# A transformer layer with 32 routed experts on one core: the last experts in another order, the accumulator's rows added after the last product, norm statistics on two engines, bounded row transfers

## The chip, the core and the metric

One core of one Trainium2 chip runs the whole layer in one launch. Its engines work side by side and meet at semaphores: TensorE (PE; its weight loads are listed as PEld), VectorE (DVE), ScalarE (ACT), GpSimd (POOL) and SyncE (SP). In this kernel SP issues the plain DMAs and POOL the indirect ones, in which a list of row numbers says which rows of a DRAM tensor are gathered or scattered. Sixteen DMA engines carry all of them. The metric is the time of one execution in microseconds (us); lower is better.

## The reference, cut to what matters

A batch of 512 tokens of width 1024 goes through a token mixer (differential attention beside a gated MLP), a LayerNorm, a mixture of experts and a second LayerNorm. The change concerns the last two:

```python
logits = xt @ w_router + b_router                      # 512 tokens, 32 experts
topv, topi = lax.top_k(logits, 4)
gates = softmax(topv)
for each expert e, for its tokens:
    h = xb @ w_up[e] + b_up[e]                         # 1024 -> 2 x 1024
    gate, lin = h[:, :1024], h[:, 1024:]
    act = (clip(lin, -7, 7) + 1) * min(gate, 7) * sigmoid(1.702 * min(gate, 7))
    y = act @ w_down[e] + b_down[e]                    # 1024 -> 1024
ffn = sum over a token's 4 experts of gate * y
x = layer_norm(2**0.25 * x + ffn, ln2_g, ln2_b)        # the output
```

There are 512 x 4 = 2048 pairs of a token and an expert.

## The kernel before, in words

**Slots.** The experts are sorted on the chip by how many tokens they have, and every rank has a fixed capacity (`CAP_STEPS`); slot 0 is a fixed expert with 128 rows. A rank of at most 64 rows is an L, of 65 to 128 an M, of 129 to 192 an H (an M of 128 rows plus an L of 64). The capacities of the 32 ranks sum to 2976 rows. `ORDER` says in which order the 31 sorted ranks follow slot 0; each letter takes the largest rank of its kind that is left. The last slot must be an L.

**An expert's work.** The up product writes PSUM tiles PG and PL, the down product PD (or X1 for the L part of an H, and for an L that stands ahead of an H). An M multiplies in three passes (L1359) of weights that ACT casts (L152) and DVE subtracts (L153) into five `ring` buffers; an L multiplies its 64 rows with the raw weights (L1345), two column halves at a time. TensorE's order is fixed by a list of chunks: up of slot n, then down of slot n-1, and at the end down of slot 30, up of slot 31, down of slot 31. Events hang between chunks: lists and gathers, transposes, activations, outputs.

**Weights.** An expert's 12 MiB come in six DMAs of 2 MiB from SP, each into one of six `raw` buffers, and a load goes out when the buffer that is six loads older has been used up.

**Rows.** `gather` (L869) and `gather_h` (L1176) fetch a slot's token rows from `x1d`; `scatter` (L1228) and `scatter_h` (L1181) add its results to `accd`, the accumulator in DRAM. Lists are as long as the capacity; entries without a token name one of 128 spare rows behind the 512 real ones, so 2976 rows are moved each way. Scatters follow one another: each waits until the one ahead has landed. The results stand in two buffers `ys` until their scatter has read them.

**The end.** When the scatter of slot 30 is issued, `summed` gathers the rows of `accd` that the last expert's tokens have (`accr`, L1625) and loads all of `accd` (`xo`, L1629, four tiles of 128 rows). `last_start` (L1690) puts `accr` into PD by two pairs of matmuls with the identity, ahead of the last down product; since that sum must be weighted right, the last expert's activations are multiplied by the gates when they are transposed (`gated`, L1295, with `last_diag`, `last_mm`, `last_gates`), and its list (`full_list`) repeats a real token in empty places. ACT forms the norm's sums (L1642) and squares (L1651) of the four `xo` tiles; DVE scales them (L1657), finishes them (L764) and SP stores them (L1665). `last_rows` then norms the last expert's rows: statistics from PD (L1696), a matmul that joins the two halves of a row (L1699), a reciprocal square root of one column in eight DVE steps, two DVE operations (L1711, L1712) and a scatter into the output (L1713), which has to come after the stores, as it overwrites rows of theirs. A loop for overflowing experts follows (L1757), here with no trips.

Of the kernel before, what the change touches and what calls it, by code (L numbers as in the profile page):

```python
# [11 lines left out]
I32 = mybir.dt.int32  # L12
# [7 lines left out]
S = 512  # L20
# [36 lines left out]
ORDER = "LMLHLMLMLMLHLMLMLMLHLMLMMLMLHLL"  # L57
# [10 lines left out]
def moe_layer(ctx, tc, x, w_in, lambda_q1, lambda_k1, lambda_q2, lambda_k2, subln_g, gmlp_ln_g,  # L68
# [786 lines left out]

    def list_cols(lp, rows, dst=None):
# [317 lines left out]
    def gather_h(idx):  # L1174
        xg = xgs[nxt("xg", len(xgs))][:, 0:512]
        nc.gpsimd.indirect_dma_start(out=xg, out_offset=None, in_=x1d_h,  # L1176
# [17 lines left out]

    def full_list(s):

        lp = xbank()[:, 0:8].rearrange("p (n c) -> p n c", n=2)
        for n in range(2):
            for i in range(NT):
                cols = tb.oh[:, i, 0:1].to_broadcast([128, 128]) if n else tb.oh[:, i]  # L1200
                nc.tensor.matmul(lp[:, n], cols, tb.R[:, i, s], start=(n == 0 and i == 0), stop=(n == 1 and i == 3))
        cols_ = words("r0", 16)
        t = view(cols_, 0, 2, 4)
        empty, gt, idx = (view(cols_, 8 + n, 1) for n in range(3))
        idx = idx.bitcast(I32)
        nc.vector.tensor_copy(t, lp)
        nc.vector.tensor_scalar(empty, t[:, 0, 1:2], -1.0, 1.0, op0=OP.mult, op1=OP.add)
        nc.vector.scalar_tensor_tensor(t[:, 0], t[:, 1], empty, t[:, 0], op0=OP.mult, op1=OP.add)
        nc.vector.scalar_tensor_tensor(idx, t[:, 0, 0:1], 2.0, bge[:, 2:3], op0=OP.mult, op1=OP.add)
        nc.vector.tensor_tensor(gt, t[:, 0, 2:3], t[:, 0, 3:4], op=OP.add)  # L1210
        return idx, gt
# [15 lines left out]
    def scatter(y, idx):  # L1227
        nc.gpsimd.indirect_dma_start(out=accd, out_offset=bass.IndirectOffsetOnAxis(ap=idx, axis=0),  # L1228
                                     in_=y, in_offset=None, compute_op=OP.add)
# [3 lines left out]
    class Slot:  # L1233
# [34 lines left out]
        def fetch(self, b):  # L1268
            if self.last:
                self.lists[b] = full_list(self.s)  # L1270
            elif self.is_half(b):
# [578 lines left out]
```

## Time and profile before

| | us |
|---|---|
| median of 3 runs | 1424.37 (1423.88 to 1429.15) |
| the profiled execution | 1428.73 |
| its span, from first to last instruction | 1427.0 |
| PE busy | 1357.9 (95% of the span) |
| DVE, ACT, POOL busy | 794.6, 600.0, 119.5 |
| mean granted clock of TensorE | 0.976 of full |

The profiled execution is 4.36 us above the median, near the slowest of the three runs; 1.73 us of it lie outside the span. Busy time is a sum over the span, and the span has two stages that matter here: some 1000 us of experts in which TensorE hardly stops, and an end of about 60 us in which it mostly does.

### The profile page before, as it was taken

What the parts mean: (1) busy time and instruction counts of PE and PEld (TensorE: products, weight loads), DVE (VectorE), ACT (ScalarE), POOL (GpSimd) and SP (SyncE); (2) the same over time, 40 slices, a digit from 0 to 9 for tenths busy, and PEclk for the clock granted to TensorE, in tenths of its full rate; (3) what the DMA queues carried; (4) which work ended last, traced back from release to release, by engine and by line L of the source; (5) the groups of instructions that cost most, each with busy time, mean ns of one, the idle gap of its engine ahead of it and who ended that gap; (6) DMA issues with size and microseconds to landing.
All of it is one profiled execution on the core that took longest, in us unless ns stands there. A gap on an engine that the chain in (4) does not pass through costs nothing. (4 is left out here: it accounts for less than half of the span.)

```text
span 1427.0 us, 16512 instructions
## 1 busy us (share of the span) xinstructions
PE 1357.9 (95%) x6242; PEld 796.2 (56%) x6242; DVE 794.6 (56%) x1221; ACT 600.0 (42%) x772; POOL 119.5 (8%) x130
## 2 busy tenths in 40 slices
PE   8999989899999999999999999999999999999973
PEld 6877777757454557464545474544454565454421
DVE  4457768658462648383536374654464775563304
ACT  3354542336252436263425263453253565362212
POOL 1000000032100010011000100110010011100010
PEclk9999999799999999999999999999999999999996
DMA  8220244579997899999888999998989999996974
GB/s 282 80 93 26 102 157 159 228 304 398 418 369 285 356 379 413 399 414 420 366 335 350 394 416 390 416 419 343 362 342 384 418 402 418 412 417 269 406 245 148
DMA packets 60114, 461.48 MB, mean 323 GB/s; under 512 B 16288, under 2 KB 19616, under 8 KB 35456
## 3 DMA queue, kind: packets, MB, share of 16 engines
q1 hardware_dynamic: 51504, 436.01, 75.3%
q0 software_dynamic: 8528, 24.39, 6.8%
q8 instruction: 50, 0.82, 0.2%
q14 instruction: 32, 0.26, 0.1%
HBM read 440.43 MB, written 19.94 MB: 323 GB/s over the span
## 5 line engine op out<-in xcount | busy, mean ns | idle before, releaser
L153 DVE TENSOR_TENSOR ring<-raw,ring 128x1024 fp32r<-128x1024 f32 (+1 forms) x400 | 466.4, 1209 | 151.4 <-ACT ring L152 150.7
L152 ACT CAST ring<-raw 128x1024 fp32r<-128x1024 f32 (+1 forms) x400 | 399.6, 1039 | 185.9 <-PE PG L1359 53.3
L1345 PE MATMUL PD<-raw,low 128*64 128x512 f32 x640 | 158.0, 609 | 0.3 <-ACT w L1332 0.2
L1359 PE MATMUL PD<-ring,bc 128*128 128x512 f32 (+7 forms) x512 | 149.0, 411 | 5.0 <-ACT ring L152 3.7
L1359 PE MATMUL PG<-ring,bc 128*128 128x512 f32 (+7 forms) x512 | 148.1, 411 | 0.6 <-ACT bc L980 0.5
L1359 PE MATMUL PL<-ring,bc 128*128 128x512 f32 (+7 forms) x512 | 147.3, 410 | 0.0
L153 DVE TENSOR_TENSOR low<-X,bc 128x512 fp32r<-128x512 f32 (+7 forms) x62 | 36.9, 595 | 189.3 <-ACT bc L152 189.2
L1345 PE MATMUL PG<-raw,low 128*64 128x512 f32 x512 | 133.6, 600 | 2.1 <-ACT low L1192 1.3
L1345 PE MATMUL PL<-raw,low 128*64 128x512 f32 x512 | 132.5, 595 | 0.0
L1359 PEld LDWEIGHTS PD<-ring,bc 128*128 128x128 f32 (+7 forms) x512 | 83.0, 174 | 60.2 <-ACT ring L152 14.3
L1359 PEld LDWEIGHTS PG<-ring,bc 128*128 128x128 f32 (+7 forms) x512 | 84.8, 172 | 47.6 <-issue 18.7
L1359 PEld LDWEIGHTS PL<-ring,bc 128*128 128x128 f32 (+7 forms) x512 | 84.8, 172 | 47.2 <-issue 18.7
L1315 ACT ACTIVATE PG<-PG 128x512 f32<-128x512 f32 (+9 forms) x33 | 25.5, 772 | 166.1 <-PE PG L1359 96.7
L152 ACT CAST bc<-X 128x512 fp32r<-128x512 f32 (+7 forms) x62 | 31.6, 510 | 141.7 <-PE X L1218 141.7
L1316 DVE TENSOR_SCALAR w<-PL 128x512 f32<-128x512 f32 (+9 forms) x32 | 29.5, 923 | 100.0 <-PE PL L1359 68.6
L1359 PE MATMUL PD<-ring,low 128*128 128x512 f32 (+7 forms) x256 | 80.9, 397 | 0.0
L1359 PE MATMUL PG<-ring,low 128*128 128x512 f32 (+7 forms) x256 | 80.7, 396 | 0.0
L1359 PE MATMUL PL<-ring,low 128*128 128x512 f32 (+7 forms) x256 | 80.1, 394 | 0.0
L1345 PEld LDWEIGHTS PD<-raw,low 128*64 128x64 f32 x640 | 38.0, 136 | 69.6 <-issue 65.0
L1345 PEld LDWEIGHTS PL<-raw,low 128*64 128x64 f32 x512 | 35.2, 136 | 61.0 <-issue 59.5
L1345 PEld LDWEIGHTS PG<-raw,low 128*64 128x64 f32 x512 | 33.4, 136 | 57.3 <-issue 48.6
L1176 POOL DMA_INDIRECT w<-x1d,small x19 | 23.1, 1217 | 498.1 <-PE PG L1359 268.7
(441 smaller groups left out, 1570.6 us busy)
## 6 DMA issues: line engine op xcount, KB each, us to landing
raw<-in_w_up_dram SPq DMA_DIRECT2D x128, 2048.0 KB, 15.6
raw<-in_w_down_dram SPq DMA_DIRECT2D x64, 2048.0 KB, 14.4
raw<-in_w_in_dram SPq DMA_DIRECT2D x8, 512.0 KB, 4.6
raw<-in_w_in_dram SPq DMA_DIRECT2D x4, 1024.0 KB, 10.4
raw<-in_w_o_dram SPq DMA_DIRECT2D x2, 2048.0 KB
raw<-in_x_dram SPq DMA_DIRECT2D x4, 512.0 KB, 6.6
raw<-in_w_in_dram SPq DMA_DIRECT2D x32, 64.0 KB, 3.1
w<-in_x_dram SPq DMA_DIRECT2D x4, 512.0 KB, 4.6
```

What stands on the lines that cost most here:

```text
L152: nc.scalar.copy(hi, src)
L153: eng.tensor_tensor(lo, src, hi.bitcast(F32), op=OP.subtract)
L1176: nc.gpsimd.indirect_dma_start(out=xg, out_offset=None, in_=x1d_h, in_offset=bass.IndirectOffsetOnAxis(ap=idx, axis=0))
L1315: nc.scalar.activation(pg, pg, AF.Silu, scale=SWIGLU)
L1316: nc.vector.tensor_scalar(l, pl, LIMIT + 1.0, 1.0 - LIMIT, op0=OP.min, op1=OP.max)
L1345: nc.tensor.matmul(P[64 * c:64 * c + 64], T[:, k], w[:, c * 512:(c + 1) * 512], start=(k == 0 and not started), stop=(k == 7))
L1359: nc.tensor.matmul(P[0:self.full, cs], x_[:, k], w_[:, cs], start=(k == 0 and n == 0), stop=(k == 7 and n == 2))
```

## The change

It does five things. The first 24 letters of `ORDER` stay; the last seven are LHLMLML, where they were MLMLHLL. The last slot becomes an ordinary L with `half_list`: no `gated`, no gate matmul, no `last_start`; its result is multiplied by its gates and `accr` is added in one DVE operation after the product. `summed` issues the loads of `xo` ahead of the gather of `accr`. The statistics of the four `xo` tiles are split: two tiles on ACT as before, two on DVE (`layer_norm_stats`, BN_STATS). The reciprocal square roots of the four tiles and of the last rows are one run of five columns, so the last four tiles are finished after the last product's statistics. And every gather and scatter gets `bounds_check` with `oob_is_err=False`, which leaves out rows whose number is past the 512 real ones (the plain scatter of the last sums into `accd` stays unbounded). Besides, results of L slots take the two halves of a `ys` buffer in turn (`y_half`).

```diff
-ORDER = "LMLHLMLMLMLHLMLMLMLHLMLMMLMLHLL"
+ORDER = "LMLHLMLMLMLHLMLMLMLHLMLMLHLMLML"
...
+    def y_half():
+        h = nxt("yh", 2) * 512
+        return y_buf()[:, h:h + 512]
...
     def gather(idx, rows):
         xg = xgs[nxt("xg", len(xgs))][0:rows]
-        nc.gpsimd.indirect_dma_start(out=xg, out_offset=None, in_=x1d,
+        nc.gpsimd.indirect_dma_start(out=xg, out_offset=None, in_=x1d, bounds_check=S - 1, oob_is_err=False,
                                      in_offset=bass.IndirectOffsetOnAxis(ap=idx, axis=0))
...
         nc.gpsimd.indirect_dma_start(out=accd_h, out_offset=bass.IndirectOffsetOnAxis(ap=idx, axis=0),
-                                     in_=y, in_offset=None, compute_op=OP.add)
+                                     in_=y, in_offset=None, compute_op=OP.add, bounds_check=2 * S - 1, oob_is_err=False)
...
             if self.last:
-                def gated(to, tp):
-                    nc.vector.tensor_tensor(to, tp, tb.last_gates.unsqueeze(1).unsqueeze(1).to_broadcast([128, 2, 2, 64]),
-                                            op=OP.mult)
-                self.aT[b] = transpose_h(self.act_rows(b), gated, self.aT[b], slice(2 * hf, 2 * hf + 2))
+                self.aT[b] = transpose_h(self.act_rows(b), nc.vector.tensor_copy, self.aT[b], slice(2 * hf, 2 * hf + 2))
...
     def summed():
 
+        tb.xo = view(words("bc", 4096), 0, 4, 1024)
+        for i in range(NT):
+            nc.sync.dma_start(tb.xo[:, i], accd[i * 128:(i + 1) * 128])
         tb.accr = xgs[0][:, 0:512]
         nc.gpsimd.indirect_dma_start(out=tb.accr, out_offset=None, in_=accd_h,
                                      in_offset=bass.IndirectOffsetOnAxis(ap=slots[-1].lists[0][0], axis=0))
-        tb.xo = view(words("bc", 4096), 0, 4, 1024)
-        for i in range(NT):
-            nc.sync.dma_start(tb.xo[:, i], accd[i * 128:(i + 1) * 128])
...
-        for i in range(NT):
+        a = slice(0, NA)
+        for i in range(NA):
             nc.scalar.activation(unused, tb.xo[:, i], AF.Copy, accum_out=sums[:, 0, i:i + 1])
...
+        for i in range(NA, NT):
+            layer_norm_stats(tb.xo[:, i], i)
...
-    def last_start():
-
-        for c in range(2):
-            nc.tensor.matmul(slots[-1].hd[64 * c:64 * c + 64], ident[:, 64 * c:64 * c + 64], tb.accr, start=True, stop=False)
 
     def last_rows(sl):
+
         zs = ring_new(0, F32)
         z, sums, idx = view(zs, 0, 512), view(zs, 1024, 512), sl.lists[0][0]
-        m, y, t, v = mv1[:, 0], rs1[:, 0:1], t1[:, 0:1], nv1[:, 0:1]
-        nc.vector.bn_stats(st1[:, 0], sl.hd)
+        m, both = mv1[:, 0], xbank()[:, 0:2]
+        nc.vector.scalar_tensor_tensor(sums, sl.hd, sl.lists[0][1], tb.accr, op0=OP.mult, op1=OP.add)
+        nc.vector.bn_stats(st1[:, 0], sums)
...
-        rsqrt(y, v, t)
-        nc.vector.scalar_tensor_tensor(z, sl.hd, mean, ln2h[:, 0], op0=OP.subtract, op1=OP.mult)
-        nc.vector.scalar_tensor_tensor(z, z, y, ln2h[:, 1], op0=OP.mult, op1=OP.add)
+        rsqrt(tb.rs, tb.nv, tb.t)
+        for i in range(NT):
+            nc.vector.scalar_tensor_tensor(tb.no[i], tb.no[i], tb.rs[:, i:i + 1], ln2[:, 1], op0=OP.mult, op1=OP.add)
+            nc.sync.dma_start(out[0][i * 128:(i + 1) * 128], tb.no[i])
+        nc.vector.scalar_tensor_tensor(z, sums, mean, ln2h[:, 0], op0=OP.subtract, op1=OP.mult)
+        nc.vector.scalar_tensor_tensor(z, z, tb.rs[:, 4:5], ln2h[:, 1], op0=OP.mult, op1=OP.add)
         nc.gpsimd.indirect_dma_start(out=out[0].rearrange("r (c f) -> (r c) f", c=2),
-                                     out_offset=bass.IndirectOffsetOnAxis(ap=idx, axis=0), in_=z, in_offset=None)
+                                     out_offset=bass.IndirectOffsetOnAxis(ap=idx, axis=0), in_=z, in_offset=None,
+                                     bounds_check=2 * S - 1, oob_is_err=False)
```

TensorE around the last expert's two products, before. PG and PL are the up product, w holds `accr` in the first of these rows and the activations in the next two, low the transposed activations, PD the down product:

```order
L1345 MATMUL PG<-raw_320_8016,low_318_7954 64x512 x2
L1345 MATMUL PL<-raw_320_8016,low_318_7954 64x512 x2
L1690 MATMUL PD<-w_76,ident_146 64x512 x2
L1191 MATMUL X_65<-ident_146,w_76 128x128 x2
L1191 MATMUL X_64<-ident_146,w_76 128x128 x2
L1345 MATMUL PD<-raw_321_8030,low_325_8106 64x512 x8
L1345 MATMUL PD<-raw_322_8040,low_325_8106 64x512 x8
L1699 MATMUL X_65<-small_77,oh_8048 128x2
```

The same place after (line numbers have moved with the edits):

```order
L1327 MATMUL PG<-raw_319_8106,low_317_8074 64x512 x2
L1327 MATMUL PL<-raw_319_8106,low_317_8074 64x512 x2
L1196 MATMUL X_64<-ident_146,w_76 128x128 x2
L1196 MATMUL X_65<-ident_146,w_76 128x128 x2
L1327 MATMUL PD<-raw_320_8117,low_326_8237 64x512 x8
L1327 MATMUL PD<-raw_321_8142,low_326_8237 64x512 x8
L1662 MATMUL X_64<-small_77,oh_8206 128x2
```

The matmuls that read `accr` are gone from between the two products; what stands ahead of the down product now are the transposes alone.

DVE at the same place, before, in two pieces. First the last small step ahead of the scaling of the four `xo` tiles, the scaling (L1657, bc is `xo`, ring the scaled tiles), and the first steps of their reciprocal square root:

```order
L1649 TENSOR_SCALAR posm_8113<-posm_8113 128x2
L1657 SCALAR_TENSOR_TENSOR ring_328_8131<-bc_8053,small_77,w_76 128x1024 x2
L1657 SCALAR_TENSOR_TENSOR ring_329_8132<-bc_8053,small_77,w_76 128x1024 x2
L1660 TENSOR_SCALAR small_77<-posm_8113 128x4
L1661 TENSOR_SCALAR small_77<-small_77 128x4
```

Then the root's last step, the finish of the tiles (L764) and the statistics of the last product in PD:

```order
L192 SCALAR_TENSOR_TENSOR small_77<-small_77 128x4
L764 SCALAR_TENSOR_TENSOR ring_328_8131<-ring_328_8131,small_77,w_76 128x1024 x2
L764 SCALAR_TENSOR_TENSOR ring_329_8132<-ring_329_8132,small_77,w_76 128x1024 x2
L1696 BN_STATS small_77<-PD 128x6
L1697 BN_AGGR small_77<-small_77 128x2
```

DVE after, again in two pieces: from the second transposed half of the activations (L1197) to the statistics of the first of DVE's two tiles,

```order
L1197 COPY low_326_8237<-X_65 128x2x2x64
L1639 TENSOR_SCALAR small_77<-posm_8204 128x2
L1640 TENSOR_SCALAR posm_8204<-posm_8204 128x2
L753 BN_STATS small_77<-bc_8182 128x6 x2
L754 BN_AGGR small_77<-small_77 128x2
```

and from the last step of the joint root of five columns to the two operations on the last expert's rows:

```order
L192 SCALAR_TENSOR_TENSOR r_324_8205<-r_324_8205 128x5
L1674 SCALAR_TENSOR_TENSOR ring_328_8261<-ring_328_8261,r_324_8205,w_76 128x1024 x2
L1674 SCALAR_TENSOR_TENSOR ring_329_8262<-ring_329_8262,r_324_8205,w_76 128x1024 x2
L1676 SCALAR_TENSOR_TENSOR ring_330_8281<-ring_330_8281,small_77,w_76 128x512
L1677 SCALAR_TENSOR_TENSOR ring_330_8281<-ring_330_8281,r_324_8205,w_76 128x512
```

Four BN_STATS and two BN_AGGR have come in ahead of the scaling; the finish of the four tiles, which stood ahead of the last product's statistics, stands behind them and behind the joint square root.

## Rows read from the trace of the kernel before

**Rows 1.** The page, parts 1 and 2: the span, TensorE's busy time, the DMA engines' tenths.

```profile
span 1427.0 us, 16512 instructions
...
PE 1357.9 (95%) x6242; PEld 796.2 (56%) x6242; DVE 794.6 (56%) x1221; ACT 600.0 (42%) x772; POOL 119.5 (8%) x130
...
DMA  8220244579997899999888999998989999996974
```

**Rows 2.** Windows of 40 us: length, busy time (instructions) by engine, granted clock, DMA share, GB/s.

```profile
520.00:560.00 40.00, 40.00 (x190) 22.50 (x187) 22.36 (x26) 20.50 (x24) 4.21 (x3) 1.00 1.01 404
...
640.00:680.00 40.00, 37.12 (x169) 18.39 (x166) 16.73 (x26) 14.52 (x19) 4.52 (x3) 0.96 1.01 420
...
920.00:960.00 40.00, 37.30 (x170) 18.27 (x166) 17.28 (x22) 15.95 (x21) 4.51 (x3) 0.96 1.01 420
```

**Rows 3.** Timeline at the first stop, ACT and TensorE: start, length, operation, idle time before.

```profile
664.71 2.94 ACT L152 CAST ring<-raw 128x1024 fp32r<-128x1024 f32 x3 [10.33 <-DMA raw<-in_w_down_dram]
...
665.81 0.71 PE L1359 MATMUL PD<-ring,bc 128*104 128x512 f32 x2 [1.69 <-ACT ring L152]
```

**Rows 4.** Windows of 2 us behind the two stops, columns as in group 2.

```profile
668.00:670.00 2.00, 2.00 (x7) 1.39 (x6) 1.93 (x7) 1.50 (x3) 0.00 (x0) 0.53 1.01 434
670.00:672.00 2.00, 2.00 (x9) 1.53 (x9) 2.00 (x3) 0.95 (x2) 1.40 (x1) 0.62 0.99 426
...
944.00:946.00 2.00, 1.44 (x5) 0.66 (x4) 2.00 (x2) 2.00 (x3) 0.00 (x0) 0.65 1.03 442
946.00:948.00 2.00, 2.00 (x6) 1.29 (x5) 1.93 (x7) 1.69 (x3) 0.00 (x0) 0.50 0.98 414
```

**Rows 5.** The page, part 3: POOL's DMA queue: packets, MB, share of 16 engines' span.

```profile
q0 software_dynamic: 8528, 24.39, 6.8%
```

**Rows 6.** Timeline at the end, columns as in group 3: TensorE.

```profile
1359.78 7.09 PE L1345 MATMUL PD<-raw,low 128*64 128x512 f32 x32 [0.20 <-ACT w L1332]
...
1394.15 1.97 PE L1690 MATMUL PD<-w,ident 128*64 128x512 f32 x4 [12.60 <-DMA w<-accd,r]
...
1397.27 7.70 PE L1345 MATMUL PD<-raw,low 128*64 128x512 f32 x32
```

**Rows 7.** Timeline at the end: DVE, ACT and POOL.

```profile
1382.99 0.43 DVE L1320 SCALAR_TENSOR_TENSOR w<-PG,w 128x256 f32<-128x256 f32 x1
...
1391.43 1.06 ACT L1642 ACTIVATE ring<-bc 128x1024 f32<-128x1024 f32 x1 [0.16 <-DMA bc<-accd]
...
1397.84 4.86 DVE L1657 SCALAR_TENSOR_TENSOR ring<-bc,small,w 128x1024 f32<-128x1024 f32 x4
...
1405.58 4.87 DVE L764 SCALAR_TENSOR_TENSOR ring<-ring,small,w 128x1024 f32<-128x1024 f32 x4
...
1410.37 0.69 DVE L1696 BATCH_NORM_STATS2 small<-PD 128x6 f32<-128x512 f32 x1
...
1414.42 0.75 DVE L1711 SCALAR_TENSOR_TENSOR ring<-PD,small,w 128x512 f32<-128x512 f32 x1
...
1416.24 0.96 POOL L1713 DMA_INDIRECT out_dram<-ring,r  x1 [3.28 <-DVEq L1758]
```

**Rows 8.** Lines L1181 (scatter) and L1665 (output stores): issue to landing.

```profile
DMA to landing us min/median/max: 4.9/11.6/12.9
...
DMA to landing us min/median/max: 2.7/2.9/2.9
```

**Rows 9.** Timeline: first and last of nine close pairs of gather and transposes; landings of L1176.

```profile
327.04 1.05 POOL L1176 DMA_INDIRECT w<-x1d,small  x1 [1.08 <-PE PG L1345]
...
334.83 0.63 PE L1218 MATMUL X<-ident,w 128*128 128x128 f32 x4
...
1305.59 0.99 POOL L1176 DMA_INDIRECT w<-x1d,r  x1 [34.03 <-issue]
...
1314.01 0.75 PE L1191 MATMUL X<-ident,w 128*128 128x128 f32 x4
...
DMA to landing us min/median/max: 3.3/8.7/10.5
```

More of the change, by code (lines that the diff above doesn't have):

```diff
@@ L1175, in gather_h @@
         xg = xgs[nxt("xg", len(xgs))][:, 0:512]
-        nc.gpsimd.indirect_dma_start(out=xg, out_offset=None, in_=x1d_h,
+        nc.gpsimd.indirect_dma_start(out=xg, out_offset=None, in_=x1d_h, bounds_check=2 * S - 1, oob_is_err=False,
                                      in_offset=bass.IndirectOffsetOnAxis(ap=idx, axis=0))
@@ L1193, in transpose_h @@
         return dst
-    def full_list(s):
-        lp = xbank()[:, 0:8].rearrange("p (n c) -> p n c", n=2)
-        for n in range(2):
-            for i in range(NT):
[L1200 to L1211, printed above, removed]
     def transpose_half(dst, src, hf, rows):
@@ L1268, in fetch @@
         def fetch(self, b):
-            if self.last:
-                self.lists[b] = full_list(self.s)
-            elif self.is_half(b):
+            if self.is_half(b):
                 self.lists[b] = half_list(self.s)
@@ L1330, in out_a @@
                 half = self.is_half(b)
-                self.y[b] = y_buf()[:, 0:512] if half else y_buf()[0:self.full]
+                self.y[b] = y_half() if half else y_buf()[0:self.full]
                 nc.scalar.activation(self.y[b], self.hd if half else PD[0:self.full], AF.Copy, scale=self.lists[b][1])
@@ L1341, in hd_taken, with half_mm @@
             return self.half and self.hd is X1
-        def half_mm(self, P, T, k, w, started=False):
+        def half_mm(self, P, T, k, w):
             for c in range(2):
                 nc.tensor.matmul(P[64 * c:64 * c + 64], T[:, k], w[:, c * 512:(c + 1) * 512],
-                                 start=(k == 0 and not started), stop=(k == 7))
+                                 start=(k == 0), stop=(k == 7))
         def half_bias(self, P, gl):
@@ L1657, in ln2_scaled @@
             nc.vector.scalar_tensor_tensor(tb.no[i], tb.xo[:, i], mv1[:, i, 0:1], ln2[:, 0], op0=OP.subtract, op1=OP.mult)
-    def ln2_out():
-        nc.vector.tensor_scalar(nv1, tb.sums[:, 2], 1.0 / D, EPS, op0=OP.mult, op1=OP.add)
-        nc.vector.tensor_scalar_mul(nv1, nv1, -0.5)
-        rsqrt(rs1, nv1, t1)
-        for i in range(NT):
-            layer_norm_out(tb.no[i], i, None, ln2[:, 1], 1)
-            nc.sync.dma_start(out[0][i * 128:(i + 1) * 128], tb.no[i])
-    def last_diag():
-        tb.last_t = words("oh", 512)
-        nc.vector.tensor_scalar(view(tb.last_t, 0, 64, p=64), ident[0:64, 0:64], slots[-1].lists[0][1][0:64], None,
-                                op0=OP.mult)
-        tb.pair = view(tb.last_t, 128, 128)
-        iv = ident.rearrange("p (c r) -> p c r", c=2)
-        nc.vector.tensor_tensor(tb.pair.rearrange("p (c r) -> p c r", c=2), iv[:, 0:1].to_broadcast([128, 2, 64]),
-                                iv[:, 1:2].to_broadcast([128, 2, 64]), op=OP.add)
-        nc.vector.tensor_scalar_mul(tb.pair, tb.pair, 0.5)
-    def last_mm():
-        tb.last_ps = xbank()[:, 0:64]
-        nc.tensor.matmul(tb.last_ps, one[0:64].to_broadcast([64, 128]), view(tb.last_t, 0, 64, p=64), start=True, stop=True)
-    def last_gates():
-        tb.last_gates = view(tb.last_t, 64, 64)
-        nc.vector.tensor_copy(tb.last_gates, tb.last_ps)
-    def last_start():
-        for c in range(2):
-            nc.tensor.matmul(slots[-1].hd[64 * c:64 * c + 64], ident[:, 64 * c:64 * c + 64], tb.accr, start=True, stop=False)
+        nc.vector.tensor_scalar(tb.nv[:, 0:NA], tb.sums[:, 2, 0:NA], -0.5 / D, -0.5 * EPS, op0=OP.mult, op1=OP.add)
+        nc.vector.tensor_scalar(tb.nv[:, NA:4], mv1[:, NA:4, 1], EPS, -0.5, op0=OP.add, op1=OP.mult)
     def last_rows(sl):
```

42 lines of the change are left out of this document (21 added, 21 removed).

## The prediction

> **What bounds the kernel now.** Read the page first: TensorE is busy for 1357.9 of 1427.0 us and the DMA engines stand at 9 tenths for most of the run [rows 1]. So two limits lie close together, and the question is where TensorE stops and for what. A table of 40 us windows answers that. Through the experts it is busy for 40.00 of 40.00 us (one such window is shown), except in two, where 2.88 and 2.70 us are missing and the DMA share is 1.01 [rows 2]. The timeline at the first of these shows the cause: ACT had been waiting 10.33 us for a down weight's DMA and TensorE waited for ACT's cast [rows 3]. A stop costs more than its length. In the four 2 us windows behind the stops the granted clock is 0.53, 0.62, 0.65 and 0.50 [rows 4], towards the lower of the two levels (1.2 of 2.4 GHz), after TensorE had stood still. The missing shares are 0.47, 0.38, 0.35 and 0.50 of 2 us, together 3.4 us.
>
> The second place is the end. Call A the moment at which the last activation is ready, 1382.99 + 0.43 = 1383.42 [rows 7]. TensorE then stands still until 1394.15, its wait of 12.60 us ended by the gather of accr, and the last product runs only from 1397.27 to 1404.97 [rows 6]. DVE scales at 1397.84, finishes the tiles from 1405.58, and only at 1410.37 turns to the last product, which had been ready for 5.4 us; the scatter of the last rows goes out at 1416.24, which is A + 32.8 [rows 7]. What follows, to 1427.0, is 10.8 us of landing and closing that the change doesn't touch.
>
> **The change, part by part.** First the end, since it is the surer part. Without last_start nothing between the two products waits for accr, and so none of the 12.6 us is owed to it. The scatter of slot 30, the loads of xo and the gather of accr now have until the end of the product to run; TensorE's last up product still lies ahead of A, and covers them. That needs a landing of the scatter (4.9 us in the quiet end, 11.6 in the median of the run [rows 8]) and then some 7 us for loads; its issue follows slot 30's down product, 15 to 17 us ahead of A (one product of this kind takes 7.09 us [rows 6], the up product is two of them). At the median landing the xo tiles would come about A + 3 instead of before A; ACT would then start its sums about 3 us later, which is the worse end here.
>
> From A on, the queue that sets the end is DVE's:
> 1. Two copies of transposed activations, 0.4 us each (L1320 takes 0.43 for as many elements [rows 7]), with TensorE's transposes between them: free at A + 1.2. TensorE starts the product then and ends it at about A + 8.3 (7.09 us at full clock [rows 6]).
> 2. The means wait for two sums on ACT, each 1.06 us and a short read-out [rows 7], say 2.5 us from A - 0.4: A + 2.1, and A + 2.4 with two small steps.
> 3. New on DVE: four BN_STATS at 0.69 us (the one row of this operation in this stage [rows 7]) and two BN_AGGR of about 0.2: 3.3 us, to A + 5.7. In return ACT loses two sums and two squares.
> 4. Scaling of four tiles, 4.86 us [rows 7]: A + 10.6; two small steps: A + 11.0. The product has been ready for 2.7 us, so DVE stays the bound here, not TensorE.
> 5. The new product-times-gate-plus-accr, priced as L1711 of the same shape, 0.75 us: A + 11.7.
> 6. Statistics, joining matmul, small steps, square root: in the trace from 1410.37 to 1414.42, 4.05 us [rows 7]; eleven steps instead of eight add three of 0.2, so 4.65 us: A + 16.4. ACT's copy of the sums, beside this path before, is gone.
> 7. The finish of four tiles, 4.87 us [rows 7], which stood ahead of the statistics and now stands behind them: A + 21.3.
> 8. The two last operations, 1.5 us, run on beside the stores; but the scatter has to wait for the last store, 0.3 us to issue and 2.9 to land [rows 8]: A + 24.5, and 0.2 for POOL: A + 24.7.
>
> The end therefore moves from A + 32.8 to A + 24.7: **8.1 us earlier**. The finish and the stores, hidden behind nothing before but DVE itself, now lie wholly on the path, which is why 12.6 us of waiting give back only 8. The worse end is 5 us, with the 3 us of late xo tiles.
>
> Second, the order of the last slots. The same 32 products are made; A depends on their sum alone as long as weights are there. H, L, L behind an M, M becomes M, L, M, L behind an H. An H leaves DMA ahead of TensorE and an L lets TensorE catch up, so the new order loses nothing that the old one had; and the last loads go out earlier. Slot 30, an M, has longer activations (1024 columns) and its down product follows an L's at once in the same PSUM tile, two short waits of under 1 us each. The H in the old place had short waits of its own. I take 0, between -1 and +2 us.
>
> Third, the bounds. The lists hold 2976 rows for 2048 pairs, so 31% of the rows are left out both ways if the bound does what its name says. POOL's queue takes 6.8% of the 16 engines' span [rows 5], 97 us; 31% of it are 30 us, spread over the experts, 30 of the page's 40 slices [rows 1] or 1070 us: 2.8% of the DMA's time. The two stops are 280 us apart; over half of that the DMA is full ([rows 2] has one such window that ends 100 us ahead of a stop), so relief before each stop is about 3.9 us, more than the 2.9 and 2.7 that are missing. With the stops goes the clock lost behind them. At best that is 2.88 + 2.70 + 3.4 = 9.0 us; at worst 0, if the skipped rows cost as much as real ones. I take **7 us**, nearer the better end, since the relief exceeds each stop but the ranks differ in how many rows they lack. [...]
>
> The trace has a gather of at most 256 KB landing after 8.7 us in the median [rows 9]. The Trainium skill, page "DMA: Bandwidth & Descriptors", section "Anatomy of one DMA — SWDGE (gpsimd) path", puts a DMA of this queue at 2.0 us plus its bytes over 436 GB/s, and so prices left-out rows by bytes alone; it gives 2.6 us for that gather, where the trace has 8.7 among the weights, so it is far off here as a latency. By the page 31% of 24.39 MB are an estimated 17 us in all and 2.3 us before each stop, which would leave short stops and make the gain of this part about 4.6 us, 1411.7 in all.
>
> The half buffers of y_half change nothing that the sum has: no wait for a y buffer stands in the windows of the stops.
>
> **The rivals.** (a) *The bounds don't relieve the DMA*: skipped rows still make descriptors or packets. For it: no row of this trace shows a bounded transfer. Against it: nothing but the name. Then the end alone gains: 1424.4 - 8.1 = 1416.3. (b) *The end gives less*: the scatter of slot 30 lands as late as the median, or M in slot 30 makes A later by 2. Gain 7 + 8.1 - 5 = 10.1, so 1414.3. (c) *Only bytes count*, as in the page's rule: 1411.7. (d) *Slower*: the bound makes POOL's row-by-row work longer, and a gather lands later by x. In nine of the 34 gathers the slot's transposes start less than 9 us after the issue (7.8 in the first, 8.4 in the last [rows 9]), with landings of 8.7 in the median; TensorE would stop nine times for x, since the transposes stand in its queue ahead of products. At x = 2.5 us (an issue of 1 us made 3.5) that is 22 us, and the whole 1424.4 - 15.1 + 22 = 1431.3, slower; with the clock lost behind each stop more. It decides from x = 1.7 us. Against it: POOL works on these for 1 us each and has nothing else to do.
>
> **How the numbers follow.** Sum: 8.1 + 7.0 + 0 = 15.1 us. Against the profiled execution, 1428.73, that is 1413.6; this execution was 4.4 us above the median of the runs, so against the median, 1424.37, it is **1409.3**. Chances: the forecast as summed, with parts between their bounds (1402 to 1414), 0.50; (a) 0.17; (b) 0.12; (c) 0.08; (d) 0.10; others 0.03. The range reaches from 9.0 + 8.1 + 1 and 4 more for a scatter that ends sooner, 1402, over (b) and (c) to (a) with the worse order, 1419. Half a per cent, 7.1 us, is about what a measurement of this kernel can tell from no change: faster means under 1417.2. The forecast, (b), (c) and some two thirds of (a) are: 0.50 + 0.12 + 0.08 + 0.11 = 0.81, less 0.03 for the tails of these cases; 0.13 for the same; 0.09 for slower, with nearly all of (d).
>
> **What would show it.** In the changed kernel TensorE's wait of 12.6 us between the last two products must be gone, and the product start about 1 us behind the last activation. DVE must run from there without a gap over 1 us to the last finish, and the scatter into the output start about 24.7 us behind A, after a wait for the last store. In 40 us windows the two stops must be gone or under 1 us, with a granted clock of 1.00 behind them. POOL's queue must carry about 17 MB instead of 24.4 and take about 4.7% of the span. The prediction is wrong in its third part if the bytes fall and the stops stay, or if the bytes stay; in its first if TensorE, not DVE, is late for the new sum at A + 11, or if xo or accr land behind A + 2.

## The result, and the profile after

The changed kernel took 1413.97 us in the median of 4 runs (1412.10 to 1415.46), the kernel before 1425.95 us in the median of 4 (1423.88 to 1429.15). The ratio is 0.9911, 95% interval 0.9893 to 0.9929: 12.0 us or 0.9% faster, within the range that was given (1402 to 1419). A second measurement gave 0.9913 (0.9895 to 0.9932). The total came out nearly as forecast (15.1 us); a good part of the reasons behind it did not, as the experiments show.

The profiled execution of the changed kernel took 1413.43 us, its span is 1411.7 us. The page, parts 1 to 3, against [rows 1] and [rows 5]:

```profile
span 1411.7 us, 16547 instructions
...
PE 1352.9 (96%) x6232; PEld 793.7 (56%) x6232; DVE 796.3 (56%) x1215; ACT 594.9 (42%) x763; POOL 120.2 (9%) x130
...
DMA  8320243579997999999978999998889997889983
...
DMA packets 60115, 454.26 MB, mean 322 GB/s; under 512 B 18580, under 2 KB 21908, under 8 KB 35456
...
q0 software_dynamic: 8528, 17.16, 4.8%
```

POOL's queue carries 17.16 MB instead of 24.39 and takes 4.8% instead of 6.8% of the span. Its number of packets, 8528, is the same to one, and the packets under 512 B have grown from 16288 to 18580 in all queues: a row that is left out still makes its packets, and it seems small ones. So the bound does what its name says for the bytes, and not for the packets.

The two windows of the stops, against [rows 2], and the 2 us windows against [rows 4] (length, busy time and instructions by engine, granted clock, DMA share, GB/s):

```profile
640.00:680.00 40.00, 37.84 (x180) 19.05 (x180) 18.10 (x27) 17.00 (x21) 5.16 (x4) 1.00 1.01 423
920.00:960.00 40.00, 39.17 (x183) 19.26 (x180) 21.83 (x26) 20.41 (x24) 5.44 (x3) 1.00 1.01 422
...
668.00:670.00 2.00, 2.00 (x13) 1.55 (x11) 1.97 (x5) 1.96 (x3) 0.96 (x1) 1.00 0.94 401
...
946.00:948.00 2.00, 2.00 (x10) 1.08 (x9) 2.00 (x3) 2.00 (x3) 0.00 (x0) 1.00 0.97 416
```

The stops are shorter, not gone: 2.16 us are missing in the first and 0.83 in the second, where 2.88 and 2.70 were. The prediction asked for under 1 us in both, which only the second meets. The clock behind them is 1.00, the higher of its two levels.

The end, against [rows 6] and [rows 7], timeline of TensorE, DVE, ACT and POOL (start, length, engine, line, operation, idle time before it and what ended that):

```profile
1362.45 1.50 POOL L1215 DMA_INDIRECT accd<-w,small  x1 [11.11 <-ACT w L1314]
1376.49 1.05 ACT L1638 ACTIVATE ring<-bc 128x1024 f32<-128x1024 f32 x1
1376.61 0.43 DVE L1302 SCALAR_TENSOR_TENSOR w<-PG,w 128x256 f32<-128x256 f32 x1
1377.54 8.78 PE L1327 MATMUL PD<-raw,low 128*64 128x512 f32 x32
...
1382.06 4.87 DVE L1650 SCALAR_TENSOR_TENSOR ring<-bc,small,w 128x1024 f32<-128x1024 f32 x4
...
1386.98 0.74 DVE L1659 SCALAR_TENSOR_TENSOR ring<-PD,small,w 128x512 f32<-128x512 f32 x1
...
1392.18 4.87 DVE L1674 SCALAR_TENSOR_TENSOR ring<-ring,r,w 128x1024 f32<-128x1024 f32 x4
...
1400.87 1.01 POOL L1678 DMA_INDIRECT out_dram<-ring,small  x1 [11.88 <-SPq L1721]
```

A, the moment at which the last activation is ready, is now 1376.61 + 0.43 = 1377.04. TensorE starts the last product 0.5 us behind it, without the wait of 12.60 us; scaling starts at A + 5.0, the new sum at A + 9.9, the finish at A + 15.1, and the last scatter into the output at A + 23.8, behind the last store. It stood at A + 32.8.

Four more rows of the kernel before are needed for what follows. They show how slot 30's rows got into the accumulator there (POOL's and ACT's timeline):

```profile
1360.00 1.56 POOL L1228 DMA_INDIRECT accd<-w,small  x1 [37.33 <-ACT w L1332]
1373.79 1.55 POOL L1181 DMA_INDIRECT accd<-k,small  x1 [12.22 <-DMA accd<-w,small]
1381.34 1.55 POOL L1181 DMA_INDIRECT accd<-w,small  x1 [6.00 <-ACT PG L1315]
...
1373.16 0.69 ACT L1332 ACTIVATE w<-PD,small 128x512 f32<-128x512 f32 x1 [12.85 <-DMA accd<-w,small]
```

Slot 30's down product had long ended when ACT took it out at 1373.16: the buffer y that it goes to was still being read by the scatter issued at 1360.00. And its own scatter went out only at 1381.34, since the scatters into the accumulator go one at a time, each when the one ahead has landed: three in a chain, the two of the slot with 192 rows (slot 29, an H) and slot 30's. The landings are at 1373.06 and 1380.62, and the next scatter starts 0.73 and 0.72 us behind them. The last scatter's row names an activation as what ended the wait, as that ended last by the profile; experiment 7, where this scatter goes out ahead of that activation, shows that it was the landing.

### The profile page after: what moved, and what is told of

Read it like the earlier page. It is cut to its first block, busy times and chain, and to the rows that moved or that the text cites. A ratio compares the mean times of both kernels' runs of the same rounds, so it can differ in the third digit from the quotient of the medians.

```text
span 1411.7 us, 16547 instructions
## 1 busy us (share of the span) xinstructions
PE 1352.9 (96%) x6232; PEld 793.7 (56%) x6232; DVE 796.3 (56%) x1215; ACT 594.9 (42%) x763; POOL 120.2 (9%) x130
## 2 busy tenths in 40 slices
DMA packets 60115, 454.26 MB, mean 322 GB/s; under 512 B 18580, under 2 KB 21908, under 8 KB 35456
## 3 DMA queue, kind: packets, MB, share of 16 engines
q0 software_dynamic: 8528, 17.16, 4.8%
## 5 line engine op out<-in xcount | busy, mean ns | idle before, releaser
L1341 PEld LDWEIGHTS PD<-ring,bc 128*128 128x128 f32 (+7 forms) x512 | 82.2, 172 | 57.8 <-ACT ring L152 12.6
L1341 PEld LDWEIGHTS PG<-ring,bc 128*128 128x128 f32 (+7 forms) x512 | 84.8, 172 | 47.7 <-issue 18.7
L1341 PEld LDWEIGHTS PL<-ring,bc 128*128 128x128 f32 (+7 forms) x512 | 84.9, 172 | 47.5 <-issue 18.7
L1298 DVE TENSOR_SCALAR w<-PL 128x512 f32<-128x512 f32 (+9 forms) x32 | 29.5, 923 | 115.2 <-PE PL L1341 73.5
L1327 PEld LDWEIGHTS PL<-raw,low 128*64 128x64 f32 x512 | 35.2, 136 | 60.9 <-issue 59.5
L1181 POOL DMA_INDIRECT w<-x1d,small x20 | 25.2, 1258 | 497.8 <-PE PG L1341 268.8
L1327 PEld LDWEIGHTS PG<-raw,low 128*64 128x64 f32 x512 | 33.5, 136 | 55.8 <-issue 49.2
```

The costliest lines, as they stand in the source:

```text
L1298: nc.vector.tensor_scalar(l, pl, LIMIT + 1.0, 1.0 - LIMIT, op0=OP.min, op1=OP.max)
L1327: nc.tensor.matmul(P[64 * c:64 * c + 64], T[:, k], w[:, c * 512:(c + 1) * 512], start=(k == 0), stop=(k == 7))
L1341: nc.tensor.matmul(P[0:self.full, cs], x_[:, k], w_[:, cs], start=(k == 0 and n == 0), stop=(k == 7 and n == 2))
```

## The experiments

In each diff the line with - is of the kernel named first, and ... stands for lines left out. Ratios are to the kernel before on the same chip, with 95% intervals. Two moments are used throughout, read from the traces: **U**, the first bias product of the last expert's up product, 0.9 us behind that product's start (the expectations call it the start), and the landing of the last scatter of a slot into the accumulator. The stretches of the stops are taken from one slot's bias product to another's (586 to 683 us and 851 to 961 us in the kernel before).

**1. The bounds alone**, on the kernel before:

```
-  indirect_dma_start(out=xg, out_offset=None, in_=x1d, ...
+  indirect_dma_start(out=xg, out_offset=None, in_=x1d, bounds_check=S - 1, oob_is_err=False, ...
...   (also gather_h, scatter, scatter_h)
```

> The kernel before with nothing changed but the bounds on its gathers and scatters of rows. Theory (the bounds lighten the DMA and so shorten the two stops): POOL's queue falls from 24.4 to about 17.2 MB with its 8528 packets unchanged, the stops at 665 and 942 us fall from 2.88 and 2.70 us to about 2.2 and 0.8, the granted clock behind them is 1.00, and the whole is 6.9 us shorter, a ratio of 0.995. Rival (the stops shrank in the changed kernel for another reason, the half buffers or a shift of the loads): bytes fall, but both stops and the low clock stay as they were, ratio 1.000 within 1 us. Rival (d), a bounded gather lands later: TensorE waits for transposes at several slots, ratio above 1.002.

Measured: 0.9956 (0.9940 to 0.9973), 6.2 us faster. The theory holds in the time and the clock (1.00), and rival (d) falls with it; 1.62 and 1.36 us are missing in the two windows, where about 2.2 and 0.8 were expected. The stretches took 93.81 and 106.12 us where the kernel before took 97.14 and 109.50. But TensorE's wait for accr also fell, which no theory had (TensorE's waits, us in total, times, longest):

```profile
PE PD L1690 <- DMA w<-accd,r: 10.3, 1, 10.3
```

**2. The changed kernel without these bounds:**

```
-  in_=y, in_offset=None, compute_op=OP.add, bounds_check=S - 1, oob_is_err=False)
+  in_=y, in_offset=None, compute_op=OP.add)
...   (also scatter_h, gather, gather_h)
```

> The changed kernel without the bounds on gathers and scatters of the slots (the last scatter into the output keeps its bound). Theory: 24.4 MB again, stops of about 2.9 and 2.7 us with a granted clock near 0.5 behind them, 6.9 us longer than the changed kernel, ratio to the kernel before 0.996 (the end's gain alone, less the order's cost). Rival (the stops went for another reason): ratio 0.991 as in the changed kernel, stops short.

Measured: 0.9966 (0.9952 to 0.9981). The stops are back (37.14 and 37.10 us of 40 in their windows), but the granted clock there is 1.00: what was lost behind the stops in the profiled execution of the kernel before isn't lost in every execution.

**3. The changed kernel with the old order**, and **4. the kernel before with the new order:**

```
-ORDER = "LMLHLMLMLMLHLMLMLMLHLMLMLHLMLML"
+ORDER = "LMLHLMLMLMLHLMLMLMLHLMLMMLMLHLL"
```

This is 3; in 4 the two lines change places.

> The changed kernel with the old order of the last slots (..MLMMLMLHLL). Theory (by the start of the last up product, which moved 5.9 us where the stops alone moved it 6.9, the new order costs about 0.9 us): last up product 0.9 us earlier than in the changed kernel, ratio to before 0.990 to 0.991, the end after the last activation unchanged. Rival (the new order is what gives the rows of the last slots time): the gather of accr or the loads of xo land behind the last activation, statistics begin up to 3 us later, ratio 0.992 or more.

> The kernel before with nothing changed but the order of the slots. Theory: the order is worth nothing or costs up to 1 us, ratio 1.000 to 1.001, with the 12.6 us wait for accr still there. Rival (the end gains from the order, since the last expert's loads go out earlier and an M stands ahead of the last): the wait for accr shrinks by several us, ratio under 0.998.

Measured: 3 gave 0.9962 (0.9948 to 0.9977), 4 gave 0.9969 (0.9951 to 0.9987). Both theories fall: the order alone is worth 4 us, and without it the changed kernel loses more than half of its gain. The order does cost what was expected ahead of the end (from the end of the second stretch to U 408.0 us instead of 406.6), but the end from U is 51.5 us long instead of 59.5. In 4 TensorE's wait for accr, with not a line of the end changed, is 4.8 us (columns as above):

```profile
PE PD L1690 <- DMA w<-accd,r: 4.8, 1, 4.8
```

In 3 the wait has merely moved to the small matmul that joins the statistics:

```profile
PE X L1662 <- DVE small L1661: 12.0, 1, 12.0
```

What these six traces have in common is the last scatter into the accumulator: the span ended 40.2 to 41.8 us after it landed, with either end. That became theory L, and the next three were chosen to break it.

**5. Bounds and order, with the old end** (1 and 4 together).

> The kernel before with the bounds and the new order of the slots, but with its old end (the rows of the accumulator put into the last product, statistics on ACT alone). Theory L (in all six kernels so far the span ends 40.2 to 41.8 us after the last scatter into the accumulator lands, whichever end is written): that scatter lands about 10 us after the last up product starts, as in the changed kernel, so the span ends within 1.5 us of the changed kernel's, ratio 0.991 to 0.993. Rival (the prediction's account, the rewritten end is worth 8.1 us by itself): ratio 0.996 to 0.997.

Measured: 0.9910 (0.9894 to 0.9927), the changed kernel's ratio without one line of its new end. Timeline of TensorE and DVE:

```profile
1381.81 1.98 PE L1690 MATMUL PD<-w,ident 128*64 128x512 f32 x4 [3.92 <-DMA w<-accd,r]
...
1385.50 4.87 DVE L1657 SCALAR_TENSOR_TENSOR ring<-bc,small,w 128x1024 f32<-128x1024 f32 x4
```

TensorE still waits 3.92 us for accr, and the time shows no cost of it: from U to the end it is 51.0 us here, 50.0 and 50.8 in two executions of the changed kernel. The span ends 29.4 us after this scaling starts, in the changed kernel 29.6.

**6. The new end alone** (2 and 3 together: old order, no bounds).

> The new end alone, with the old order of the slots and without the bounds of the slots' gathers and scatters (the last scatter into the output keeps its bound). Theory L: the last scatter into the accumulator still waits for the two of the slot of 192 rows ahead of it and lands some 18.7 us after the last up product starts, so the end moves by less than 1.5 us, ratio 0.999 to 1.001, and TensorE's 12.6 us wait for accr is replaced by DVE's wait for the tiles of the sum. Rival (the prediction's account): last scatter into the output 8 us earlier, ratio 0.994.

Measured: 0.9987 (0.9975 to 0.9999), 1.9 us: a little under the 0.999 that theory L had, and far from the rival's 0.994. Timeline of TensorE, POOL and DVE:

```profile
1377.89 7.09 PE L1327 MATMUL PD<-raw,low 128*64 128x512 f32 x32
...
1376.06 1.55 POOL L1186 DMA_INDIRECT accd<-w,small  x1 [6.25 <-ACT PG L1297]
...
1387.34 0.17 DVE L1639 TENSOR_SCALAR small<-posm 128x2 f32<-128x2 f32 x1 [8.91 <-ACT ring L1638]
...
1391.87 4.87 DVE L1650 SCALAR_TENSOR_TENSOR ring<-bc,small,w 128x1024 f32<-128x1024 f32 x4
...
1410.88 1.01 POOL L1678 DMA_INDIRECT out_dram<-ring,small  x1 [12.06 <-SPq L1721]
```

Here the last product runs at once and is done 6.9 us before DVE even starts scaling. A is 1377.40, so scaling starts at A + 14.5, where it started at A + 14.4 in the kernel before, and the last scatter into the output stands at A + 33.5. The wait has gone over to DVE: it stands still for 8.91 us until ACT has the sums of the first tiles, which are loaded behind the last scatter's landing.

**7. One scatter of the chain taken away**, in the kernel before (64 rows of slot 29 are missing from the output):

```
         for b in range(self.nparts):
+            if self.is_half(b) and self is slots[N - 3]:
+                continue
             (scatter_h if self.is_half(b) else scatter)(self.y[b], self.lists[b][0])
```

> The kernel before with one scatter left out, the one of the half part (64 rows) of the last slot of 192 rows; these rows are missing from the output. Theory L (the scatters into the accumulator go one at a time, each waiting for the one ahead to land): the chain of three becomes two, the last lands 6 to 7 us earlier, the wait for accr falls from 12.6 to about 6 us, ratio 0.995 to 0.996. Rival (something else in the order, the late loads of the last expert or the slot's own product, holds the last scatter): it is issued as late as before, wait 12 us, ratio 1.000.

Measured: 0.9954 (0.9935 to 0.9972), 6.6 us, the ratio that theory L has. In the trace the landing moves by 5.5 us (6 to 7 expected) and the wait for accr falls to 7.2 (about 6 expected). ACT, POOL and the wait of TensorE:

```profile
1374.67 0.69 ACT L1332 ACTIVATE w<-PD,small 128x512 f32<-128x512 f32 x1 [13.04 <-DMA accd<-w,small]
...
1375.64 1.55 POOL L1181 DMA_INDIRECT accd<-w,small  x1 [12.76 <-ACT w L1332]
...
PE PD L1692 <- DMA w<-accd,r: 7.2, 1, 7.2
```

The last scatter follows ACT's copy at once, and lands 13.2 us after U instead of 18.7. What still holds it is the other half of the chain, the y buffer: ACT's copy waits until the scatter that reads it has landed.

The landing and what follows it, in all these traces (us; "scaling" is the start of DVE's scaling of the tiles):

| kernel | landing − U | landing to scaling | scaling to end | landing to end | U to end |
|---|---|---|---|---|---|
| before | 18.7 | 11.6 | 29.2 | 40.8 | 59.5 |
| new end alone (6) | 18.8 | 11.0 | 29.5 | 40.6 | 59.4 |
| bounds (1) | 16.5 | 11.5 | 29.3 | 40.8 | 57.3 |
| bounds, new end (3) | 16.3 | 12.0 | 29.8 | 41.8 | 58.2 |
| one scatter less (7) | 13.2 | 11.7 | 29.2 | 40.9 | 54.1 |
| order, new end (2) | 11.9 | 11.9 | 29.6 | 41.4 | 53.3 |
| order (4) | 11.2 | 11.3 | 29.1 | 40.4 | 51.5 |
| bounds, order (5) | 9.7 | 11.9 | 29.4 | 41.3 | 51.0 |
| changed kernel | 9.8 | 10.6 | 29.6 | 40.2 | 50.0 |

**8. The changed kernel once more**, and **9, 10. with bounds on gathers alone and on scatters alone:**

```
-  in_=y, in_offset=None, compute_op=OP.add, bounds_check=S - 1, oob_is_err=False)     (9; scatter_h too)
+  in_=y, in_offset=None, compute_op=OP.add)
...
-  indirect_dma_start(out=xg, out_offset=None, in_=x1d, bounds_check=S - 1, oob_is_err=False, ...  (10; gather_h too)
+  indirect_dma_start(out=xg, out_offset=None, in_=x1d, ...
```

> The changed kernel itself, once more, beside the three that follow, on one chip. Expected: ratio 0.991 as before; the two stretches that hold the stops (from the bias product of the slot at 586 us to that at 680, and from 861 to 954) 93 to 94.5 us long each as in every kernel with bounds so far, where those without took 95.1 us and more; the span ends 40 to 42 us after the last scatter into the accumulator lands.

> The changed kernel with bounds on the gathers only; the slots' scatters write all their rows again. Theory (bytes: POOL's queue carries a row once in a gather and its scatter has to read and add it, so the scatters are the larger half of what the bounds save): about half of the 7 MB saved, stops in between (stretches of 94 to 95.5 us each), the last scatter into the accumulator lands 11 to 12 us after the last up product starts instead of 9.8, ratio 0.994 to 0.996. Rival (the gathers alone matter, since TensorE waits for what they fetch): ratio 0.991.

> The changed kernel with bounds on the slots' scatters only; the gathers fetch all their rows again. Theory: about half of the bytes saved, stops in between, but the last scatter lands 9.8 us after the last up product starts as in the changed kernel, ratio 0.992 to 0.994. Rival (the gathers alone matter): stops of 95 us and more, ratio 0.995 or above.

Measured: 0.9913 (0.9895 to 0.9932), 0.9934 (0.9918 to 0.9950) and 0.9938 (0.9923 to 0.9953). 9 carries 20.77 MB and 10 20.60, always 8528 packets: each side is half of the bytes, and each ratio lies about half-way between those without bounds (0.9966) and with both; 9 came out slightly better than expected. Of the DMA engines' time the scatters are the larger part: the queue's share is 6.7% in experiment 2, 6.1% in 9 and 5.5% in 10. The last scatter lands at U + 11.3 in 9 and at U + 9.4 in 10, so the end's share comes from the scatters, as expected. The expected lengths of the stretches did not hold: counted as there, the first took 95.4 us in 8, all bounds in place, 93.7 in 9 and 95.7 in 10, the second 93.2 to 93.7 in all three. From one execution to the next such a stretch moves by over a microsecond, so a single one proves little.

**11. A tile of the output on ACT and GpSimd**, three tiles' sums on ACT:

```
-    NA = 2
+    NA = 3
...
+            if i == 0:
+                nc.scalar.activation(tb.no[i], tb.xo[:, i], AF.Identity, bias=tb.sums[:, 1, i:i + 1])
+                nc.gpsimd.tensor_tensor(tb.no[i], tb.no[i], ln2[:, 0], op=OP.mult)
+                continue
...
-        for i in range(NT):
+        for i in (1, 2, 3, 0):
+            if i == 0:
+                nc.scalar.activation(tb.no[i], tb.no[i], AF.Copy, scale=tb.rs[:, i:i + 1])
+                nc.gpsimd.tensor_tensor(tb.no[i], tb.no[i], ln2[:, 1], op=OP.add)
```

> The changed kernel with three tiles' statistics on ACT instead of two, and the first tile of the output scaled and finished on ACT and GpSimd instead of DVE. Theory (DVE's queue sets the end in the changed kernel from 1.2 us behind the last activation on): the new sum starts when the product is ready, 0.7 us earlier, and the finish takes three tiles instead of four, 1.2 us less: 1.5 to 2 us earlier, ratio 0.9895. Rival (tiles of the sum land too late for a shorter queue to matter, or GpSimd is slower over its tile than DVE over the other three): the last store goes out as late or later, ratio 0.991 to 0.993.

Measured: 0.9929 (0.9910 to 0.9947), no gain; the last scatter into the output moved from A + 23.8 to A + 27.6. POOL and DVE:

```profile
1382.51 2.35 POOL L1652 TENSOR_TENSOR ring<-ring,w 128x1024 f32<-128x1024 f32 x1 [12.60 <-ACT ring L1651]
1391.54 3.38 POOL L1680 TENSOR_TENSOR ring<-ring,w 128x1024 f32<-128x1024 f32 x1 [4.65 <-ACTq L1729]
...
1382.58 2.30 DVE L1655 TENSOR_SCALAR r<-posm 128x3 f32<-128x3 f32 x1
...
1390.24 5.76 DVE L1682 SCALAR_TENSOR_TENSOR ring<-ring,r,w 128x1024 f32<-128x1024 f32 x3
```

GpSimd isn't only slow over its tile: DVE's finish of three tiles takes 5.76 us beside it, where four take 4.87 alone in the changed kernel, and an operation on three columns, where one on two takes 0.16 us there, takes 2.30.

**12. The tiles finished and stored ahead of the last rows' statistics**, with a root of their own:

```
+        scaled(0)
+        scaled(1)
+        ln2_mean(slice(2, 3))
+        layer_norm_stats(tb.xo[:, 3], 3)
+        scaled(2)
+        scaled(3)
...
+        rsqrt(tb.rs[:, 0:4], tb.nv[:, 0:4], tb.t[:, 0:4])
...   (finish and stores of the four tiles now ahead of the copy of both)
-        rsqrt(tb.rs, tb.nv, tb.t)
+        rsqrt(tb.rs[:, 4:5], v, t)
```

> The changed kernel with its end in another order: ACT sums three tiles, DVE scales two of them before the others' statistics are there, takes the tiles' root apart from the last rows' and finishes and stores the four tiles while the last rows' statistics are joined. Theory (DVE's queue sets the end, and the finish with the landing of its stores is what stands on the path): the last scatter into the output goes out 21.9 us after the last activation instead of 23.8, not held by a store, 1.9 us less than the changed kernel. Rival (DVE's extra root of 2.2 us takes back what the hidden stores give): 23 to 24.5 us, no difference.

Measured: 0.9927 (0.9912 to 0.9941), no gain; the last scatter into the output at A + 26.8, beyond what the rival had. DVE and POOL:

```profile
1379.61 2.48 DVE L1652 SCALAR_TENSOR_TENSOR ring<-bc,small,w 128x1024 f32<-128x1024 f32 x2 [3.73 <-DMA w<-in_ln_g_dram]
...
1400.60 1.01 POOL L1687 DMA_INDIRECT out_dram<-ring,small  x1 [10.31 <-SPq L1730]
```

DVE was ready 3.73 us before the norm's weights were there: they are loaded behind the tiles of the sum, which are loaded behind the last scatter. So in the changed kernel too DVE's queue alone doesn't set the start of scaling (its weights landed at 1381.41, 0.65 us ahead of the scaling). It is the same chain once more. Behind scaling the theory failed too: the last scatter was held by a store after all. The finish ends 15.1 us behind the start of scaling, where it ends after 15.0 us in the changed kernel, but the stores, issued from 1391.19 on, landed after 4.9 to 5.0 us each, where those of the changed kernel take 2.7 to 2.9; no run shows why. Neither version beats the changed kernel.

## Why the prediction came out right, and where its reasons were wrong

The bounds, the order and the end, each there or not, make eight kernels, of which one is the kernel before. The mean of the four differences that each part makes, in ratios and in us of 1425:

| part | forecast | measured as the mean of four differences |
|---|---|---|
| bounds | −7 us | −0.0046, −6.5 us |
| order | 0 (−1 to +2) | −0.0037, −5.3 us |
| new end | −8.1 us | −0.0002, −0.3 us |

Each ratio is known to about 0.0016 to either side, so such a mean to 0.0016 × √8 / 4 = 0.0011, 1.6 us. The sum is 12.1 us, what was measured for the whole. "New end" here is all that is neither order nor bounds, the half buffers too, which no run has by themselves. That the total lies near the forecast is luck: the end was priced 7.8 us too high and the order 5.3 us too low, and the two errors largely cancel.

1. **The end: right in its times, wrong in its cause.** The steps from A on held one by one: copies and product, scaling, new sum at A + 9.9 (forecast 11.0), finish at A + 15.1 (16.4), last scatter at A + 23.8 (24.7). The product took 8.78 us instead of 7.09, with a granted clock of 0.51 and 0.64 in the windows 1378 to 1380 and 1380 to 1382 us, behind two windows in which TensorE was busy for 1.18 and 1.41 us of 2, and DVE hid that. One sign that the prediction had named against itself was there: accr landed at A + 2.5 and the last tile of the sum at A + 2.8, behind A + 2. What failed is the sentence ahead of them: that without last_start the scatter of slot 30 "now" has the up product to run, since "its issue follows slot 30's down product, 15 to 17 us ahead of A". In the kernel before it went out at 1381.34, 2 us ahead of A, and the row was there to be read. In the changed kernel it does go out 14.6 us ahead of A, but the removal of last_start doesn't move it (experiment 6); the order does (experiment 4), since with M, L, M, L no slot with two scatters stands right ahead of the last ones. The wait of 12.6 us was a symptom: TensorE and DVE waited for the same landing. In the kernel before, the norm's weight that scaling needs landed at 1396.83, 8.6 us after its issue behind the tiles, and scaling started at 1397.84, so with these landings the end without last_start could have started it 1.0 us earlier at most.
2. **Why the new end gives nothing that can be told from zero** (0.3 us, known to 1.6). From scaling on both ends do nearly the same work on DVE, and the table has 29.1 to 29.4 us for the old one and 29.5 to 29.8 for the new one. The new end saves a root of its own for the tiles (from 1402.97 to 1405.58 in the kernel before) and pays for it with the landing of the stores, which the last scatter now waits for. The prediction compared its chain with A + 32.8 as a whole and didn't split that into what comes before scaling and what after; split, the second part would have shown 18.4 us in the kernel before (1397.84 to 1416.24) and by its own steps 19.0 (A + 5.7 to A + 24.7).
3. **The order: mis-sized by its place.** It was weighed for TensorE alone, and there it costs 1.4 us, within the bounds given. What it does to the queue of scatters wasn't looked at.
4. **The bounds: the size held, its make-up didn't.** Over five executions without and seven with them the stretches of the stops differ by 1.8 and 3.1 us (means 95.73 and 108.85 against 93.92 and 105.74), 4.9 us in all instead of 7. About 2 us more come from a place that wasn't forecast, the last scatter's earlier landing (U + 18.7 to 16.5 by experiment 1, 11.9 to 9.8 by experiment 2). The DMA's relief was as priced: the queue took 97 us of the engines' time before (6.8% of 1427.0) and 68 after (4.8% of 1411.7), 29 us less where 30 were forecast. What failed is the step from there to 3.9 us before each stop, more than a stop's length: 1.8 and 3.1 us came of it. The 3.4 us for the clock were read from one execution. In experiment 6 stops as long (2.78 and 2.69 us missing in the windows of 40 us) leave the clock at 1.00, in experiment 7 the second one (2.86) brings it to 0.50. Windows of 2 us behind the second stop, columns as above, first of experiment 6, then of 7. In 6 TensorE had been busy for 0.29 and 1.44 us of 2 in the two windows ahead of this one; in 7 the clock fell from 946 us on, behind two windows with 0.99 and 0.69:

```profile
942.00:944.00 2.00, 2.00 (x12) 1.56 (x11) 1.93 (x7) 1.52 (x3) 0.00 (x0) 1.00 0.98 414
```

```profile
948.00:950.00 2.00, 2.00 (x6) 1.17 (x6) 1.93 (x7) 1.32 (x2) 0.22 (x1) 0.50 1.03 442
```

5. **The rivals.** (a) is half true: skipped rows keep their packets, and the DMA is relieved all the same. (b) fell: the scatter of slot 30 landed 5.6 us ahead of A, and the last scatter into the output came 9.0 us nearer to A, though by order and bounds. (c), bytes alone, isn't told apart from the forecast: each half of the bytes was worth about half of the gain, and its 4.6 us for the stops are nearest to the 4.9 measured. The Trainium skill ("DMA: Bandwidth & Descriptors", "Anatomy of one DMA — SWDGE (gpsimd) path") prices a DMA of this queue at about 2.0 us and its bytes over 436 GB/s, so left-out rows by their bytes alone. As to what the stops gave, the runs agree with the 4.6 us worked out from it; as to the engines' time they don't (29 us less, where its estimate is 17), nor as to latency (2.6 us for a gather of 256 KB, against the 8.3 and 8.7 us of the next sentence). (d) falls: the bounded gathers of half slots take 1.07 us of POOL in the median against 1.02, and land after 8.3 us against 8.7 [rows 9]. The line of these gathers in the changed kernel (durations in ns, then landings in us):

```profile
L1181 POOL DMA_INDIRECT w<-x1d,small x20: 1007/1068/1992, 291.8 to 1301.7; - x20
...
DMA to landing us min/median/max: 7.3/8.3/10.3
```

6. **The time.** Against the profiled execution 15.1 us were forecast and 15.3 came: 2.8 and 3.9 us in the two stretches and 9.5 from U to the end, less 1.0 for the longer way from the second stretch to U; the little that is left lies elsewhere. Against the median 12.0 came. The profiled execution of the kernel before had a low clock behind its stops, which is in the sum; that most of its other executions didn't is likely by the traces without bounds (in two of five a stop cost clock) and by their mean clocks (0.976 here, 0.976 to 0.984 in the 28 executions beside experiments 1 to 4), but not shown, as only this one was traced.

What stays open: why the clock falls behind some stops and not behind others of the same length, and whether a shorter way from the last scatter's landing to scaling (the 10.6 to 12 us for loads of the sum and of the norm's weights) would show in the time. Neither was tried.

## What to carry to other kernels

When an engine waits a long time for a DMA, follow the wait back to what held that DMA's issue, before pricing the removal of the waiting instruction: scatters that add into one tensor go one at a time, and the last in the chain may set the end for every engine at once. A total that comes out right doesn't show that its parts were right; switching each part on and off, alone and with the others, tells. And a loss that is read from one execution (a low clock here) is worth checking in a second one before it is put into a sum.

## What the hardware showed that wasn't expected

- A gather or scatter with a bound keeps its packets and drops its bytes: 8528 packets with and without, 24.39 to 17.16 MB, 6.8% to 4.8% of the engines' time; packets under 512 B rose from 16288 to 18580.
- A scatter that adds 64 rows as 128 half rows landed after 4.9 us in the kernel before [rows 8], when the last weights had landed, and one of 72 whole rows after 9.0 us in the changed kernel, beside the last weight loads; it is the landing, not the 1.6 us of POOL, that a chain of them costs.
- DVE and GpSimd hold each other up (experiment 11, one execution): three tiles took DVE 5.76 us beside a GpSimd TENSOR_TENSOR, against 3.65 (three quarters of 4.87) without it, and GpSimd's own took 3.38 us where its first took 2.35. The Trainium skill ("GPSIMD Engine Reference", "1. Specifications") says that GpSimd's access to SBUF is shared with VectorE, with contention when a DVE instruction has two SBUF inputs, as the scaling and the finish have, or runs in a 2-port perf mode. The run agrees as to the finish; the operation on three columns has only one such input and was held too, and no run here shows in which mode it ran.
